# Ordering the later experts of a mixture-of-experts layer by token count on the chip, half of them with 32 places, four to a unit, their weights addressed from registers

## The chip, the cores and the metric

The kernel runs on one core of one Trainium2 chip. The metric is the device time of one execution in microseconds (us). The kernel before took 2621.86 us (median of 3 runs, 2621.36 to 2623.19).

## What is computed

A decoder layer on 512 tokens of 2048 channels in float32: two mixers, then a mixture of experts, then a gated per-layer embedding and a norm. The change is in the mixture of experts. Of the reference, what matters there:

```python
# N_GROUPS = 4, EXPERTS_PER_GROUP = 8, TOP_K = 2, D_EXPERT = 512
gi = jnp.argmax(logits_grp, axis=-1)                   # one group of 8 experts for each token
top_vals, top_idx = lax.top_k(le, TOP_K)               # two experts of that group
weights = p_sel[:, None] * jax.nn.softmax(top_vals, axis=-1)
expert_ids = gi[:, None] * EXPERTS_PER_GROUP + top_idx
# for each expert e, on the tokens xb that chose it:
hmid = jax.nn.silu(xb @ w_gate[e]) * (xb @ w_up[e])    # 2048 x 512 each
yb = hmid @ w_down[e]                                  # 512 x 2048
acc.at[idx].add(yb * wt[:, None])
```

All 32 experts' weights, 12 MiB each, are read from device memory once. With the reference's own inputs its routing gives these token counts, sorted within each group of eight: 54 49 47 45 39 38 35 31; 46 35 33 30 30 26 24 20; 52 34 33 32 32 31 28 26; 34 29 20 20 20 19 19 13.

## The kernel before, in words

The expert stage is `experts` (L1223). Every expert has 64 places for tokens (`SLOTS`); two experts form a pair, whose places fill the 128 columns of a stationary operand. For each pair there are these steps on TensorE (PE):

- `gather` (L1084) makes a one-hot matrix `G` from the tokens' ranks and multiplies the hidden state `h` by it, in a high and a low part (`ghi`, `glo`, made by ScalarE and VectorE), for two pairs (256 columns) at a time. It is a generator; one call of `next` is a **turn**, 16 matmuls of 128x256.
- `up` (L1127) multiplies the gathered tokens by `w_gate` and `w_up`, in four steps `b`, each with four weight tiles of 1 MiB. Its matmuls alternate between the two experts, 64 columns of the array each. After each `b` it calls a *window*, in which other work is put: a turn of the next gather, or a `scatter`.
- `places` (L1143) makes scale factors and the transposed one-hot matrix `GT`; `hidden` (L1163) forms the gated product; `hidden_turned` (L1171) transposes it.
- `down` (L1188) multiplies by `w_down` (8 tiles of 1 MiB), and `weighed` (L1180) splits the result in a high and a low part.
- `scatter` (L1211) adds the result back into `h`, 8 matmuls of 128x512 per step `cb`.

PE runs the program in the order written (`manual_schedule`); the other engines' order is the scheduler's. Two pairs go together: up, up, down, down. The weights come through `weight_stream` (L1029): `fill_stream` (L1064) issues each 1 MiB load on SP's queue as soon as a place is free, in the order of use. There are 16 places; four serve once, twelve (`RING` 11 and `LEFT` 1) are used again and again. `next_weights` (L1077) gives a place back when its tile is handed to PE, and the next load into it waits on SP until PE has read it. Near the end three places are kept back (`self.keep = 3`) for `project_p` (L1457), the embedding's product, whose own three inputs also lie in such places.

`count_overflow` (L1315) counts the tokens of each expert. Where one has more than its places, `overflow` (L1355) works the rest off in blocks, in a loop that sits just before the last `up` (L1267). All engines read the number of blocks (L1290) after the first two `up`. With the counts above there are none. The last pair's `down_by_columns` (L1201) alternates with `scatter` and `last_norm` (L1502); then comes `tail`.

Of the kernel before, what the change touches and what calls it, by code (L numbers as in the profile page):

```python
# [12 lines left out]
I32 = mybir.dt.int32  # L13
# [12 lines left out]
SLOTS = 64  # L26
D_POOL = 1024
# [35 lines left out]
class Layer:  # L63
# [867 lines left out]
    def router(self, pp, pm):  # L931
# [59 lines left out]
        for t in range(NT):  # L991
# [29 lines left out]
        self.aux = self.p_rt.tile([P, NT, N_EXP // 2, 3], F32, name="aux", bufs=1)  # L1021
        tt(self.aux[:, :, :, 1:3].rearrange("p t (g h) i -> p t g h i", g=4),
           og[:, :, :, None, None].to_broadcast([P, NT, 4, 4, 2]),
           wj[:, :, None, 0, :].rearrange("p t o (h i) -> p t o h i", i=2).to_broadcast([P, NT, 4, 4, 2]), op=OP.mult)
        nc.vector.tensor_copy(self.aux[:, :, :, 0], bc(rstd[:, :, None], N_EXP // 2))
        self.Mb = Mb


    def weight_stream(self):  # L1029

        a = self.a
        wp = a["w_ple_proj"][0].rearrange("(k p) (h c) -> h p k c", p=P, h=2)
        for p in range(0, N_EXP, 4):
            for q in (p, p + 2):
                for b in range(4):
                    for w in (a["w_gate"][0], a["w_up"][0]):
                        for i in range(2):
                            yield "w", w[q + i, b * T:(b + 1) * T, :].rearrange("(p j) c -> p j c", j=4), (4, T)  # L1040
                if q == N_EXP - 6:
                    yield "p", a["p"][0, 0].rearrange("(t p) c -> p t c", p=P), (NT, 256)
                    yield "p", wp[0], (2, 1024)
                if q == N_EXP - 4:
                    yield "p", wp[1], (2, 1024)
            for q in (p, p + 2):
                for k in range(4):
                    for i in range(2):
                        if q < N_EXP - 2:
                            yield "w", a["w_down"][0, q + i, k * P:(k + 1) * P, :], (D,)  # L1050
                        else:
                            yield "w", a["w_down"][0, q + i, :, k * T:(k + 1) * T].rearrange("(k p) c -> p k c", p=P), (4, T)
# [31 lines left out]
    def gather(self, pp, n):  # L1084


        nc, half = self.nc, n % 2
        home = self.p_late if half else pp
        G = home.tile([P, NT, 4, SLOTS], F32R, name=f"G{half}", bufs=1)
        m = NT if n else 1  # L1090
        for t in range(0, NT, m):
            nc.vector.tensor_tensor(G[:, t:t + m], self.slot[:, None, None, :].to_broadcast([P, m, 4, SLOTS]),  # L1092
                                    self.rank[:, t:t + m, 4 * n:4 * n + 4, None].to_broadcast([P, m, 4, SLOTS]),
                                    op=OP.is_equal)
        xe = []
        Gf = G.rearrange("p t e s -> p t (e s)")
# [8 lines left out]
        def turns():  # L1105
            ready = [parts(0), parts(1)]
            for k0 in range(0, KD, 2):
                ps = self.bank("dl")
                for i in range(2):
                    hi, lo = ready.pop(0)  # L1110
                    p = ps[:, 256 * i:256 * i + 256]
                    for t in range(NT):
                        nc.tensor.matmul(p, hi[:, t, :], Gf[:, t, :], start=t == 0, stop=False)  # L1113
                        nc.tensor.matmul(p, lo[:, t, :], Gf[:, t, :], start=False, stop=t == NT - 1)  # L1114
                if k0 + 2 < KD:
                    ready = [parts(k0 + 2), parts(k0 + 3)]
                x2 = home.tile([P, 2, 256], F32, name=f"xe{half}", bufs=KD // 2)
                for i in range(2):
                    k = k0 + i
                    nc.scalar.activation(x2[:, i, :], ps[:, 256 * i:256 * i + 256], AF.Copy,  # L1120
                                         scale=self.g_moe4[:, k // 4, k % 4:k % 4 + 1])
                    xe.append(x2[:, i, :])
                yield

        return G, xe, turns()

    def up(self, q, xe, window):  # L1127

        nc = self.nc
        c0 = (q % 2) * P  # L1130
        out = [self.bank("mm") for _ in range(2)]
        for b in range(4):
            for ps in out:
                ws = [self.next_weights() for i in range(2)]
                for j in range(4):
                    k = 4 * b + j
                    for i in range(2):
# [5 lines left out]
    def places(self, q, G):  # L1143

        nc, pp = self.nc, self.p_late
        c0 = (q % 2) * P
        Gf = G.rearrange("p t e s -> p t (e s)").bitcast(F32)
        pt = self.bank("dl")
        pa = self.bank("dl")
        for t in range(NT):  # L1150
            nc.tensor.matmul(pa[:, 0:3], Gf[:, t, c0:c0 + P], self.aux[:, t, q, :], start=t == 0, stop=t == NT - 1)
        for t in range(NT):
            nc.tensor.transpose(pt[:, t * P:(t + 1) * P], Gf[:, t, c0:c0 + P], self.ident)
        sc = pp.tile([P, 4], F32, name="sc", bufs=2)
        nc.vector.tensor_scalar(sc[:, 0:1], pa[:, 0:1], 0.5, None, op0=OP.mult)
        nc.vector.tensor_tensor(sc[:, 1:2], sc[:, 0:1], pa[:, 0:1], op=OP.mult)
        nc.vector.tensor_copy(sc[0:64, 2:3], pa[0:64, 1:2])
        nc.vector.tensor_copy(sc[64:128, 2:3], pa[64:128, 2:3])
        GT = pp.tile([P, T], F32R, name="GT", bufs=2)
# [28 lines left out]
    def down(self, hT, sc, window):  # L1188

        nc = self.nc  # L1190
        out = [self.bank("mm") for _ in range(4)]
        for k in range(4):
            window(k)
            ws = [self.next_weights() for i in range(2)]
            for cb in range(4):
                for i in range(2):
                    nc.tensor.matmul(out[cb][64 * i:64 * i + 64, :], hT[:, k, 64 * i:64 * i + 64],  # L1197
                                     ws[i][:, cb * T:(cb + 1) * T], start=k == 0, stop=k == 3)
        return [self.weighed(ps, sc) for ps in out]

    def down_by_columns(self, hT, sc, cb):  # L1201
        nc = self.nc
        ws = [self.next_weights() for i in range(2)]
        ps = self.bank("mm")
        for k in range(4):
            for i in range(2):
                nc.tensor.matmul(ps[64 * i:64 * i + 64, :], hT[:, k, 64 * i:64 * i + 64], ws[i][:, k, :],  # L1207
                                 start=k == 0, stop=k == 3)
# [14 lines left out]
    def experts(self, pp):  # L1223
        G, xe, turns = self.gather(pp, 0)
        next(turns)
        next(turns)
        left = None
        state = {}
        for n in range(N_EXP // 4):
            last = n == N_EXP // 4 - 1  # L1230
            if n == 0:
                state["turns"] = iter(())
            elif not last:
                state["next"] = self.gather(pp, n + 1)
                state["turns"] = state["next"][2]
            else:
                self.keep = 3
                state["turns"] = iter(())

            def first(b):  # L1240
                if n == 0:
                    next(turns, None)
                    next(turns, None)
                else:
                    if not last:
                        next(state["turns"], None)
                    self.scatter(b, left[0], left[1][b])
                if last:
                    if b == 0:
                        state["turns"] = self.project_p(pp)  # L1250
                    for _ in range((2, 3, 3, 4)[b]):
                        next(state["turns"])
                if b == 3:
                    state["a"] = self.places(2 * n, G)
                    if last:
                        state["b"] = self.places(2 * n + 1, G)

            out = self.up(2 * n, xe, first)
            GTa, sca = state["a"]
            hm = self.hidden(out, sca)  # L1260
            if n == 0:
                state["next"] = self.gather(pp, 1)
                state["turns"] = state["next"][2]
            if last:
                state["hTa"] = self.hidden_turned(hm)
# [4 lines left out]
            def second(b):  # L1270
                if b == 0 and not last:
                    state["hTa"] = self.hidden_turned(hm)
                if not last:
                    next(state["turns"], None)
                if n == 0:
                    next(state["turns"], None)
                if last:
                    for _ in range(3 if b else 1):
                        next(state["turns"], None)
                if b == 3 and not last:  # L1280
# [426 lines left out]
```

## Time and profile before

| what | value |
|---|---|
| median of 3 runs | 2621.86 us |
| the profiled execution's own time | 2616.97 us |
| its span, first to last instruction | 2614.9 us |
| PE busy | 2511.0 us (96%), 12358 matmul records |
| VectorE (DVE) busy, ScalarE (ACT) busy | 1148.9 us (44%), 776.7 us (30%) |
| expert stage, first `up` to last `down_by_columns` | 1361.3 to 2408 us of the span |
| read from device memory | 545.01 MB, mean 211 GB/s over the span |

Busy shares are means over the whole span, in which stages with different limits follow one another, and a busy PE is not PE at its peak, since the ends of pipelined matmuls are modelled. The expert stage is therefore read from windows, from the order of matmuls in time and from what the DMA queue waits for.

### The profile page before, as it was taken

Reading aid. Unit: us, or ns where it says so; the run is one execution under the profiler, and the core shown is the slowest. Engines: PE = TensorE matmul, PEld = TensorE weight load, DVE = VectorE, ACT = ScalarE, POOL = GpSimd, SP = SyncE. Lnnn points to the kernel's source line nnn. Section 1 sums busy time; section 2 is a strip of 40 time slices with the busy share of each in tenths; the row PEclk is TensorE's granted clock in tenths of the full one; section 3 lists DMA queues with packets and bytes.
Section 4 is the critical chain, followed back from the end, with each engine's and each line's share of the span. In section 5 each row is a group of like instructions: output and inputs, shape, how many; then the busy total and the mean of one; then the engine's idle time right before and its main releaser. Section 6 shows DMA issues by size and latency. Waiting matters only on the chain. (4 is left out here: it accounts for less than half of the span.)

```text
span 2614.9 us, 30940 instructions
## 1 busy us (share of the span) xinstructions
PE 2511.0 (96%) x12358; PEld 1720.5 (66%) x12358; DVE 1148.9 (44%) x2042; ACT 776.7 (30%) x1308; POOL 83.8 (3%) x92
## 2 busy tenths in 40 slices
PE   7999999999999999999989899999999999989998
PEld 6788888887888888877754444444444444444788
DVE  6475766765222233345453343333334333315435
ACT  4233242424222222234434222223222222113323
POOL 1001110100000000000000000000000000000001
PEclk9999999999999999999989999999999999999999
DMA  5222223234333333373237799999999999977222
GB/s 153 81 79 73 79 58 94 68 97 125 97 97 97 97 97 97 97 292 126 81 138 283 324 378 416 379 422 374 422 377 421 384 421 376 401 307 278 97 97 97
DMA packets 197975, 554.16 MB, mean 212 GB/s; under 512 B 30378, under 2 KB 127043, under 8 KB 148035
## 3 DMA queue, kind: packets, MB, share of 16 engines
q1 hardware_dynamic: 194610, 543.61, 55.4%
q10 hardware_dynamic: 2640, 4.33, 0.5%
q0 software_dynamic: 576, 4.19, 0.4%
q8 instruction: 99, 1.62, 0.2%
q14 instruction: 50, 0.40, 0.0%
HBM read 545.01 MB, written 7.08 MB: 211 GB/s over the span
## 5 line engine op out<-in xcount | busy, mean ns | idle before, releaser
L1138 PE MATMUL ps_mm<-wm,xe 128*64 128x512 f32 x2048 | 454.7, 597 | 10.6 <-DMA wm<-in_w_gate_dram 5.3
L99 PE MATMUL ps_mm<-n1h,whi 128*128 128x512 f32 x1120 | 450.4, 402 | 0.9 <-ACT whi L94 0.9
L101 PE MATMUL ps_mm<-n1h,wlo 128*128 128x512 f32 x1120 | 437.3, 391 | 1.7 <-DVE wlo L95 1.6
L100 PE MATMUL ps_mm<-n1l,whi 128*128 128x512 f32 x1120 | 437.1, 390 | 0.0
L95 DVE TENSOR_TENSOR wlo<-raw,whi 128x1024 fp32r<-128x1024 f32 x206 | 254.4, 1235 | 412.5 <-ACT whi L94 401.4
L94 ACT CAST whi<-raw 128x1024 fp32r<-128x1024 f32 x206 | 216.3, 1050 | 545.1 <-PE ps_mm L100 538.9
L1138 PEld LDWEIGHTS ps_mm<-wm,xe 128*64 128x64 f32 x2048 | 141.8, 137 | 287.0 <-issue 264.1
L95 DVE TENSOR_TENSOR glo<-h,ghi 128x512 fp32r<-128x512 f32 x128 | 137.2, 1096 | 361.1 <-ACT ghi L94 352.8
L94 ACT CAST ghi<-h 128x512 fp32r<-128x512 f32 x128 | 139.6, 1134 | 425.3 <-PE ps_dl L1113 314.2
L101 PEld LDWEIGHTS ps_mm<-n1h,wlo 128*128 128x128 f32 x1120 | 210.0, 188 | 47.3 <-DVE wlo L95 2.5
L99 PEld LDWEIGHTS ps_mm<-n1h,whi 128*128 128x128 f32 x1120 | 210.8, 188 | 40.3 <-ACT whi L94 1.3
L100 PEld LDWEIGHTS ps_mm<-n1l,whi 128*128 128x128 f32 x1120 | 210.9, 188 | 38.7
L1197 PE MATMUL ps_mm<-wm,hmT 128*64 128x512 f32 x960 | 218.8, 601 | 9.0 <-DVE eidx L1353 6.9
L1221 DVE TENSOR_TENSOR h<-h,ps_dl 128x512 f32<-128x512 f32 x256 | 160.2, 682 | 98.7 <-PE ps_dl L1219 95.9
L1197 PEld LDWEIGHTS ps_mm<-wm,hmT 128*64 128x64 f32 x960 | 66.5, 137 | 135.2 <-issue 130.0
L1113 PE MATMUL ps_dl<-G,ghi 128*128 128x256 f32 x512 | 134.2, 298 | 1.9 <-DVE G L1092 0.9
L1114 PE MATMUL ps_dl<-G,glo 128*128 128x256 f32 x512 | 128.5, 288 | 5.2 <-DVE glo L95 5.2
L1113 PEld LDWEIGHTS ps_dl<-G,ghi 128*128 128x128 f32 x512 | 99.2, 194 | 42.4 <-issue 38.9
L1218 PE MATMUL ps_dl<-yhi,GT 128*128 128x512 f32 x256 | 107.8, 421 | 14.0 <-ACT xe L1120 14.0
L1114 PEld LDWEIGHTS ps_dl<-G,glo 128*128 128x128 f32 x512 | 99.2, 194 | 7.1 <-DVE glo L95 6.9
L101 PE MATMUL ps_mm<-whi,ml 128*128 128x512 f32 x256 | 100.0, 391 | 2.1 <-DVE ml L95 2.1
L1219 PE MATMUL ps_dl<-ylo,GT 128*128 128x512 f32 x256 | 100.7, 393 | 0.0
(402 smaller groups left out, 3262.4 us busy)
## 6 DMA issues: line engine op xcount, KB each, us to landing
wm<-in_w_gate_dram SPq DMA_DIRECT2D x128, 1024.0 KB, 8.7
wm<-in_w_up_dram SPq DMA_DIRECT2D x128, 1024.0 KB, 10.2
wm<-in_w_down_dram SPq DMA_DIRECT2D x128, 1024.0 KB, 9.5
raw<-in_w_in_dram SPq DMA_DIRECT2D x144, 512.0 KB, 3.7
raw<-in_w_out_dram SPq DMA_DIRECT2D x32, 512.0 KB, 3.7
wm<-in_w_ple_gate_dram SPq DMA_DIRECT2D x16, 1024.0 KB, 5.0
raw<-in_w_up_dn_dram SPq DMA_DIRECT2D x16, 512.0 KB, 3.5
raw<-in_w_up_pool_dram SPq DMA_DIRECT2D x16, 512.0 KB, 3.6
```

The costliest lines, as they stand in the source:

```text
L94: i = self.nc.scalar.copy(hi, src)
L95: return i, self.nc.vector.tensor_tensor(lo, src, hi.bitcast(F32), op=OP.subtract)
L99: mm(ps, whi, xhi, start=start, stop=False)
L100: mm(ps, whi, xlo, start=False, stop=False)
L101: mm(ps, wlo, xhi, start=False, stop=stop)
L1113: nc.tensor.matmul(p, hi[:, t, :], Gf[:, t, :], start=t == 0, stop=False)
L1114: nc.tensor.matmul(p, lo[:, t, :], Gf[:, t, :], start=False, stop=t == NT - 1)
L1138: nc.tensor.matmul(ps[64 * i:64 * i + 64, :], xe[k][:, c0 + 64 * i:c0 + 64 * i + 64], ws[i][:, j, :], start=k == 0, stop=k == KD - 1)
L1197: nc.tensor.matmul(out[cb][64 * i:64 * i + 64, :], hT[:, k, 64 * i:64 * i + 64], ws[i][:, cb * T:(cb + 1) * T], start=k == 0, stop=k == 3)
L1218: nc.tensor.matmul(pc, GT[:, s], yh, start=True, stop=False)
L1219: nc.tensor.matmul(pc, GT[:, s], yl, start=False, stop=True)
L1221: nc.vector.tensor_tensor(d, d, pc, op=OP.add)
```

## The change

Experts 0 to 7 stay as they were. The experts 8 to 31 are sorted within their group by token count on the chip (`order_experts`, in place of `count_overflow`); `rank` and `aux` are permuted alike. The four with most tokens keep 64 places and form two pairs; the other four get 32 places each and form one unit of four. So there are 13 units (10 pairs and 3 of four) where there were 16 pairs. The weights of a sorted expert are addressed by a register that SP loads from `order`. Gathers are remade: two of 256 columns for units 0 to 3, one of 256 for units 4 and 5 and one of 128 for unit 6, then two of 384 for units 7 to 9 and 10 to 12. The order becomes up 0, up 1, down 0, up 2, down 1, and so on to up 12, down 11, down 12; a table (`plan`) says in which window a turn runs. Blocks beyond an expert's places are counted against its own 64 or 32. The overflow loop now sits between up 12 and down 11.

```diff
+LIGHT = 32
+FIRST = 8
+    def units(self):
+        u = [(0, 1), (2, 3), (4, 5), (6, 7)]
+        for g in range(FIRST, N_EXP, 8):
+            u += [(g, g + 1), (g + 2, g + 3), (g + 4, g + 5, g + 6, g + 7)]
+        return u
+    def expert(self, s):
+        if s < FIRST:
+            return slice(s, s + 1)
+        if s not in self.chosen:
+            e = self.nc.values_load(self.order[0:1, s:s + 1], engines=[mybir.EngineType.SP],
+                                    min_val=FIRST, max_val=N_EXP - 1)
+            self.chosen[s] = bass.ds(e, 1)
+        return self.chosen[s]
...
+        def ups(u):
+            for b in range(4):
+                for w in ("w_gate", "w_up"):
+                    for s in u:
+                        yield "w", rows(w, s, slice(b * T, (b + 1) * T)).rearrange("(p j) c -> p j c", j=4), (4, T)
...
-    def up(self, q, xe, window):
+    def up(self, u, xe, c0, window):
-        nc = self.nc
-        c0 = (q % 2) * P
+        nc, w = self.nc, P // len(u)
...
-                ws = [self.next_weights() for i in range(2)]
+                ws = [self.next_weights() for _ in u]
                 for j in range(4):
                     k = 4 * b + j
-                    for i in range(2):
-                        nc.tensor.matmul(ps[64 * i:64 * i + 64, :], xe[k][:, c0 + 64 * i:c0 + 64 * i + 64],
+                    for i in range(len(u)):
+                        nc.tensor.matmul(ps[w * i:w * i + w, :], xe[k][:, c0 + w * i:c0 + w * i + w],
                                          ws[i][:, j, :], start=k == 0, stop=k == KD - 1)
-            window(b)
+                window(b, h)
...
+        put(g0, *[("half", 0, b) for b in range(3)], *ups(0, range(3)))
+        put(start_2(), *ups(1), *downs(0))
+        put(start_pairs(4), *downs(1, (1, 2, 3)), *ups(3), *downs(2, (0,)))
+        put(start_light(6), *downs(2, (1, 2, 3)), *ups(4), *downs(3, (0,)))
+        for u in (7, 10):
+            put(start_all(u), *downs(u - 3, (3,)), *ups(u - 1), *downs(u - 2, (0, 1, 2)))
...
+            out = self.up(units[u], *xe[u], in_up)
+            hm[u] = self.hidden(out, at[u][1])
+            if u == 0:
+                self.order_experts(pp)
+            if u == 1:
+                self.n_blocks = self.nc.values_load(self.n_over[0:1, 0:1], min_val=0, max_val=N_EXP)
...
+            if u:
+                y[u - 1] = self.down(units[u - 1], hT[u - 1], at[u - 1][1], in_down)
...
+        def put(x):
+            tt(tmp, sel, x[:, :, None, :].to_broadcast(sh), op=OP.mult)
+            red(x, tmp, axis=AX.X, op=OP.add)
...
+        put(eights(cn))
+        put(eights(self.eidx))
+        self.order = rt.tile([P, N_EXP], I32, name="order", bufs=1)
+        nc.vector.tensor_copy(self.order, self.eidx)
+        for t in range(NT):
+            put(eights(self.rank[:, t, :]))
+            put(self.aux[:, t, 1:4, 1:9])
```

How the instructions move, at three places. **VectorE, after the first `up`.** `th` is the gated product, `sc` the scale factors, `G` the one-hot matrix, `glo` the low part for a gather, `key`, `tmp`, `pos` and `sel` the sort's tiles. Before:

```order
L1092 TENSOR_TENSOR G_10760<-slot,rank 128x1024
L1155 TENSOR_SCALAR sc<-ps_dl 128x1
L1156 TENSOR_TENSOR sc<-sc,ps_dl 128x1
L1157 COPY sc<-ps_dl 64x1
L1158 COPY sc<-ps_dl 64x1
L1167 SCALAR_TENSOR_TENSOR th_10756<-th_10756,ps_mm 128x512
L1168 SCALAR_TENSOR_TENSOR th_10756<-th_10756,sc,ps_mm 128x512
L95 TENSOR_TENSOR glo<-h,ghi 128x512 x14
```

Now:

```order
L1422 COPY cn<-ps_mm 128x32
L1217 SCALAR_TENSOR_TENSOR th_10773<-th_10773,sc,ps_mm 128x512
L1430 SCALAR_TENSOR_TENSOR key<-cn,prio 128x24
L1124 TENSOR_TENSOR G<-slot,rank 128x4x256
L1434 TENSOR_TENSOR tmp_10791<-key 128x192
L1436 TENSOR_REDUCE pos<-tmp_10791 128x24
L1438 TENSOR_TENSOR sel<-pos,eidx 128x192
L1442 TENSOR_TENSOR tmp_10791<-sel,cn 128x192
L1443 TENSOR_REDUCE cn<-tmp_10791 128x24
L1442 TENSOR_TENSOR tmp_10791<-sel,eidx 128x192
```

The first `glo` of the second gather stood right behind the gated product; now most of the sort and the whole count stand between, 21 instructions on 192 elements a partition and 25 smaller ones.

**SP, at the count of blocks.** Before:

```order
L1073 DMA wm<-in_w_down_dram 128x2048 x12
L1290 TENSOR_LOAD n_over
L1291 COMPARE_AND_BRANCH
L1344 DMA h_dram<-h 128x2048 x4
L1291 UNCONDITIONAL_BRANCH x2
L1290 ISA x2
L1073 DMA wm<-in_w_down_dram 128x2048 x4
```

Now:

```order
L1105 DMA wm<-in_w_down_dram 128x2048 x8
L1105 DMA wm<-in_w_gate_dram 128x2048 x2
L1105 DMA wm<-in_w_up_dram 128x2048 x2
L1376 TENSOR_LOAD n_over
L1377 COMPARE_AND_BRANCH
L1479 DMA h_dram<-h 128x2048 x4
L1377 UNCONDITIONAL_BRANCH x2
L1376 ISA x2
L1044 TENSOR_LOAD order
L1044 ISA x2
```

The last two rows come 14 times in a row there, ahead of the 45th weight load; the other ten register loads stand later, each ahead of its expert's first load. Every load of a sorted expert's tile has one further instruction of SP ahead of it.

**PE, a step of `up`.** Before, a pair's step with a turn of a gather behind it:

```order
L1138 MATMUL ps_mm<-wm,xe_11434 64x512 x4
L1138 MATMUL ps_mm<-wm,xe_11502 64x512 x4
L1138 MATMUL ps_mm<-wm,xe_11434 64x512 x4
L1138 MATMUL ps_mm<-wm,xe_11502 64x512 x4
L1113 MATMUL ps_dl<-G_12115,ghi 128x256
L1114 MATMUL ps_dl<-G_12115,glo 128x256
```

Now, the first step of unit 6 behind the end of down 4:

```order
L1160 MATMUL ps_dl<-G,glo 128x384
L1247 MATMUL ps_mm<-wm,hmT 64x512 x8
L1187 MATMUL ps_mm<-wm,xe_12017 32x512 x32
L1159 MATMUL ps_dl<-G,ghi 128x384
L1160 MATMUL ps_dl<-G,glo 128x384
```

A step of four experts has 32 matmuls of 32x512 where a pair's has 16 of 64x512, over twice the weights. In all, `up` and `down` go from 1536 matmuls to 960 of 64 columns and 576 of 32; gathers from 1024 matmuls to 768; scatters from 512 to 416.

## Rows read from the trace of the kernel before

**Rows 1.** The page's 40 equal slices: DMA's busy tenths and what it moved.

```profile
DMA  5222223234333333373237799999999999977222
GB/s 153 81 79 73 79 58 94 68 97 125 97 97 97 97 97 97 97 292 126 81 138 283 324 378 416 379 422 374 422 377 421 384 421 376 401 307 278 97 97 97
```

**Rows 2.** Windows: span, busy by engine (records), then clock, DMA share, GB/s.

```profile
1490.00:1500.00 10.00, 10.00 (x44) 4.13 (x44) 3.79 (x7) 0.00 (x0) 0.00 (x0) 1.00 1.01 421
2000.00:2100.00 100.00, 95.89 (x494) 45.60 (x496) 37.77 (x55) 28.78 (x41) 0.00 (x0) 1.00 0.97 397
```

**Rows 3.** Waits of SP's queue, 1480 to 2260 us: us in total, times, longest.

```profile
SPq L1073 <- PE ps_mm L1138: 424.6, 96, 9.5
SPq L1073 <- PE ps_mm L1197: 221.4, 53, 6.7
```

**Rows 4.** Timeline of PE (start us, us, work): steps of down and up.

```profile
1495.74 3.65 PE L1197 MATMUL ps_mm<-wm,hmT 128*64 128x512 f32 x16
...
1501.38 3.65 PE L1197 MATMUL ps_mm<-wm,hmT 128*64 128x512 f32 x16
1505.03 7.09 PE L1138 MATMUL ps_mm<-wm,xe 128*64 128x512 f32 x32
1516.78 7.09 PE L1138 MATMUL ps_mm<-wm,xe 128*64 128x512 f32 x32
...
1552.69 1.05 PE L1151 MATMUL ps_dl<-aux,G 128*128 128x3 f32 x8 [0.42 <-DVE h L1221]
...
1554.16 7.09 PE L1138 MATMUL ps_mm<-wm,xe 128*64 128x512 f32 x32
...
1563.68 7.09 PE L1138 MATMUL ps_mm<-wm,xe 128*64 128x512 f32 x32
1572.81 7.09 PE L1138 MATMUL ps_mm<-wm,xe 128*64 128x512 f32 x32
```

**Rows 5.** The same timeline, where the first up begins.

```profile
1361.29 7.09 PE L1138 MATMUL ps_mm<-wm,xe 128*64 128x512 f32 x32
```

**Rows 6.** The same timeline, inside a turn of a gather.

```profile
1512.50 0.28 PE L1114 MATMUL ps_dl<-G,glo 128*128 128x256 f32 x1
1512.62 0.28 PE L1113 MATMUL ps_dl<-G,ghi 128*128 128x256 f32 x1
```

**Rows 7.** Timeline of DVE and PE at the count of blocks.

```profile
1460.49 0.19 DVE L1325 COPY cn<-ps_mm 128x32 f32<-128x32 f32 x1
...
1465.16 0.18 DVE L1353 CAST eidx<-ei 128x32 f32<-128x32 int32 x1
...
1466.05 8.84 PE L1197 MATMUL ps_mm<-wm,hmT 128*64 128x512 f32 x32 [6.89 <-DVE eidx L1353]
```

**Rows 8.** DVE by line and shape in the router, 1340 to 1362 us: busy, mean ns.

```profile
L976 DVE TENSOR_TENSOR le<-lg,ge 128x128 f32<-128x128 f32 x1 | 0.3, 284 | 0.0
```

**Rows 9.** PE's wait for the weighed output when an up follows a down.

```profile
PEld ps_mm L1138 <- DVE ylo L1185: 10.5, 6, 1.9
```

**Rows 10.** SP by line, ns min/median/max: a register load, what follows it, a weight load.

```profile
L1290 SPq TENSOR_LOAD <-n_over x1: 480/480/480, 1465.2 to 1465.2; - x1
L1290 SPq FUSED_REGOPS  x1: 191/191/191, 1466.2 to 1466.2; - x1
...
L1073 SPq DMA_DIRECT2D wm<-in_w_down_dram x128: 327/378/3400, 1423.9 to 2378.3; - x128
```

**Rows 11.** Timeline of PE at the end of the stage, and the page's span.

```profile
2295.64 6.18 PE L1138 MATMUL ps_mm<-wm,xe 128*64 128x512 f32 x28
...
2320.09 4.19 PE L1138 MATMUL ps_mm<-wm,xe 128*64 128x512 f32 x12 [5.32 <-DMA wm<-in_w_gate_dram]
...
2371.57 7.09 PE L1197 MATMUL ps_mm<-wm,hmT 128*64 128x512 f32 x32
...
span 2614.9 us, 30940 instructions
```

**Rows 12.** DMA issues of the page: count, KB each, median us to landing.

```profile
raw<-in_w_in_dram SPq DMA_DIRECT2D x144, 512.0 KB, 3.7
```

More of the change, by code (lines that the diff above doesn't have):

```diff
@@ L1223, in experts @@
     def experts(self, pp):
[L1224 to L1236, printed above, removed]
-                self.keep = 3
[L1238 to L1265, printed above, removed]
@@ new lines, in experts, with gathered, spots @@
+        units = self.units()
+        last = len(units) - 1
+        xe, G = {}, {}
+        def gathered(us, G_, c0, homes):
+            parts, turns = self.gather(pp, G_, c0, homes)
+            us = iter(us)
+            for p, (_, w) in zip(parts, homes):
+                for c in range(0, w, P):
+                    xe[next(us)] = (p, c)
+            return turns
+        def spots(us, first=False):
+            widths = [(P // len(units[us[0]]), 4)]
+            if len(us) == 3:
+                widths.append((LIGHT, 4))
+            G_ = self.spots(pp, units[us[0]][0], widths, first)
+            for i, u in enumerate(us):
+                G[u] = (G_, i * P)
+            return G_
@@ new lines, in experts, with in_up @@
+        hm = {}
+        for u in range(len(units)):
+            def in_up(b, h):
+                if h == 0:
+                    turn("half", u, b)
+                    return
+                if u == 1 and b == 0:
+                    turned(0)
+                turn("up", u, b)
+                if u >= 2:
+                    self.scatter(b, at[u - 2][0], y[u - 2][b])
+                if u == last:
+                    for _ in range(3):
+                        next(rest)
+                if b == 3 and u not in at:
+                    place(u)
+                    if u in (0, 2):
+                        place(u + 1)
+            if u == last:
+                rest = self.project_p(pp)
+            if u == last - 1:
+                self.keep = 3
+            out = self.up(units[u], *xe[u], in_up)
[4 more added lines that the diff above has]
+                self.n_blocks = self.nc.values_load(self.n_over[0:1, 0:1], min_val=0, max_val=N_EXP)
+                with self.tc.If(self.n_blocks > 0):
+                    self.save_h()
+            if u == last:
+                turned(u)
@@ L1268, in experts @@
                     self.overflow(pp)
[L1270 to L1280, printed above, removed]
-                    state["b"] = self.places(2 * n + 1, G)
@@ L1298, in experts, with in_down @@
-            ya = self.down(state["hTa"], sca, third)
-            if not last:
-                yb = self.down(state["hTb"], scb, lambda k: self.scatter(k, GTa, ya[k]))
-                left = GTb, yb
-                G, xe, _ = state["next"]
+            def in_down(k):
+                if k == 2 and u < last:
+                    turned(u)
+                turn("down", u - 1, k)
+                if k == 1 and u < last and len(units[u + 1]) == 4:
+                    place(u + 1)
+                if u == last:
+                    for _ in range(3):
+                        next(rest, None)
@@ L1325, in count_overflow @@
[L1325 to L1327 removed]
+        tt(cn, cn, self.own, op=OP.subtract)
+        ts(nb, cn, 0.0, None, op0=OP.is_gt)
+        for m in range(1, T // SLOTS):
             stt(nb, cn, float(m * SLOTS), nb, op0=OP.is_gt, op1=OP.add)
```

271 lines of the change are left out of this document (164 added, 107 removed).

## The prediction

> **What bounds the kernel now.** I read the page's slices first [rows 1]: from the 22nd slice DMA is over 90% busy through the expert stage and moves 374 to 422 GB/s in turns. Windows say what that alternation is [rows 2]: where the queue is never empty it moves 421 GB/s at share 1.01, over 100 us 397 at 0.97, with PE busy 96%. So one 1 MiB tile (1.0486 MB), a chunk from here on, costs at best 1.0486/0.421 = 2.49 us, and in the middle of the stage 2.64. What holds the rest back is in SP's waits [rows 3]: of 780 us SP waits 646 for PE to have read a tile, so the places are always full and PE sets the pace. PE's steps tell why [rows 4]. A pair's `up` step of four chunks lasts 7.0 us (7.09 with the last matmul's tail); with a turn behind it 1572.81 - 1563.68 = 9.13, so a turn is 2.1; two chunks of `down` with a scatter last 1501.38 - 1495.74 = 5.6, so a scatter is 5.6 - 3.5 = 2.1; an `up` step with both 1516.78 - 1505.03 = 11.75. `places` is 1554.16 - 1552.69 = 1.5, the turned product some 0.4. Two pairs cost 48 chunks: DMA's 119.5 us against PE's 47 (up with both) + 36.5 (up with turns) + 3 + 28 + 8.4 (two downs, a scatter) + 0.8 = 124. The stage is therefore bound by PE by a few per cent, and weight traffic is close beneath. That is the key: PE can lose as much work as it likes, the stage cannot go below 2.49 us a chunk.
>
> **The change, part by part.** I lay the new program along the trace's own time. The stage begins at 1361.3 [rows 5], with 16 chunks loaded.
>
> Units 0 to 5 are still pairs. Up 0: 4 x 7.0, six turns, two `places`: 28 + 12.6 + 3 = 43.6, until 1404.9. Then the sort. Before, the count alone kept DVE from 1460.5 to 1465.2 and PE idle 6.9 us; after that PE's first 32 matmuls took 8.84 instead of 7.09, 1.8 more [rows 7]. Now 46 instructions stand ahead of the second gather's `glo`: 21 on 192 elements, at least the 0.28 us of 128 elements [rows 8] and, in proportion, at most 0.43, and 25 at 0.16 (4.7 us for 29): 10 to 13 us, and 3 us for G and the gated product. Up 1's first step covers 7.4 of it, so PE waits 6 to 9; the cover can also be better, since the first parts run meanwhile: bounds 0 and 15, I take 9, plus 1.8. Up 1: 28 + 0.4 + 8.4 + 10.8 = 47.6, until 1452.5; the read of the block count some 1; down 0: 14 + 0.4 + 8.4 = 22.8, until 1476.3 with 40 chunks used. Before, that point was 1482.4, so the sort is paid by what the count no longer costs.
>
> SP's 14 register loads there cost 0.48 + 0.19 us each [rows 10] and a little between: 10 to 12 us without a new load. The twelve chunks ahead hold over 20 us of PE's work, and PE is the slower here, so I cost this at nothing; without that cover it would be 10. Later, a further 0.19 us for each load makes 0.38 + 0.19 = 0.57 of SP's time a chunk, far under 2.49.
>
> Until unit 6 every `up` follows a `down`. An `up` needs two banks that `weighed` still reads: 10.5/6 = 1.75 us each [rows 9]; a `down` behind an `up` I give 0.5. Then: up 2: 28 + 8.4 + 3 + 1.75 = 41.2; down 1: 14.4 + 6.3 = 20.7; up 3: 47 + 1.75 = 48.8; down 2: 14.4 + 8.4 = 22.8; up 4: 47 + 1.5 + 1.75 = 50.3; down 3: 16.5; four half microseconds 2. A turn of 128 columns I price like one of 256, since matmuls follow each other at 0.12 us there [rows 6] and each still loads 128 columns of weights. Sum 202.3, until 1678.6 with 112 chunks used. That is 2.81 us a chunk, slower than now, because units 4 to 6 gather in two passes. The twelve places are then full, two in flight: 122 landed.
>
> From here DMA sets the pace. Three units (pair, pair, four) are 96 chunks, 239 us of DMA. PE needs 28 + 28 + 31 for up, 14 + 14 + 15.5 for down, 25 for three scatters, eight turns of 384 columns at 16 x 0.175 = 2.8 (between 0.12 a matmul and a scatter's 2.1/8 = 0.26), 22, and 10 for the rest: some 188. The four's step of four chunks I take at 3.9 us, which is 32 pairs of load and matmul at the 0.12 us of a turn [rows 6]; the ends are 3.5 (four experts in the time of two, per matmul half the price) and 7.0 (only two at once). PE's waits of up to 6 us between a four's steps bring the slow clock with them, 1.8 us at each restart as above [rows 7]; with twelve places it hides under the loads. Up 12's last chunk is the 363rd: 241 x 2.49 = 600, so 2278.7.
>
> **The end.** In up 12 only six or seven places turn over (three kept or taken for `project_p`, its inputs in two or three). PE frees four at a time while three are under way: I add 4 us (0 to 31, the upper end if each of the eight steps had 3.9 us with no load under way). The last step: 3.9, until 2286.6. Before, PE needed from the end of up 14's matmuls (2301.8) to 2320.1 for window, count of places and loop [rows 11]; now there are two `places` and one product less, 18.3 - 3.0 - 1.4 = 14. From 2320.1 to the end of that pair's `down`, 2378.7, it was 58.6, of which the `up` 28 that no longer lies behind the loop: 30.6. From there to the end of the span 2614.9 - 2378.7 = 236.2, which stays: seven of the 24 chunks left are under way at the loop, the rest lands in some 50 us while PE has as much to do. 2286.6 + 14 + 30.6 + 236.2 = 2567.4.
>
> **Sum.** The span falls by 47.5 us. Against the profiled execution's own 2616.97 that is 2569.5; the median of the runs lies 4.9 above that execution, so I forecast **2574 us**. Without the sort's wait (11), the four's places (4) and the bank waits (9) it would be 2550.
>
> A rule of the skill speaks against any gain at all. Rows 2 show 421 GB/s into one core. The Trainium skill (DMA: Bandwidth & Descriptors, Specifications) gives a limit of about 358 GB/s for one core's share of device memory. (The skill's HBM Reference adds that a core alone measures about 425.) By the limit a chunk would cost 2.93 us, the 241 chunks 106 us more, and the kernel would end at 2680, slower than before; the trace disagrees, since it holds 421 where the queue is full.
>
> **The rivals.**
> 1. *Fours run two at a time.* For it: the trace has only two experts side by side. Against it: those two do overlap fully, 32 matmuls of 0.59 us in 7.09 us [rows 4]. Units 6 and 9 still hide it (56 + 8 + 11 = 75 of 80 us); in unit 12 a step then takes 7.0 + 4.5 to refill, or 7.0 + 6.3 with a window's work, 12.4 instead of 10.2 on average, 18 us, and four steps of `down_by_columns` 3.1 more each: 2574 + 31 = 2605. The Trainium skill (TensorE: Matmul & The Clock Gate, Part 3) reports 3.07 times for four tiles, which would make the step 4.6 us and the sum some 4 us more; no run so far shows it.
> 2. *DMA does not hold 421.* If 397 over 100 us [rows 2] is DMA's own pace and not PE's, a chunk costs 2.64 and 241 of them 36 more: 2610. Against it: SP's waits name PE.
> 3. *An expert of a light half gets more than 32 tokens* and the overflow loop runs. It decides at the 33rd token. Third group's fifth count is exactly 32; the others are 30 and 20. One block loads 64 tiles of 256 KB in three places; a 512 KB load takes 3.7 us to land [rows 12], so 64 x 3.7/3 = 79 at least and 237 one at a time. I take 79: 2653, slower than before.
> 4. *Loads by register are slow to issue.* If SP needs more than 2.49 us a chunk it becomes the bound; from 2.69 the gain is gone. The longest issue in the trace took 3.4 us [rows 10], which on all 241 chunks would be 2793, but the median is 0.38.
>
> **How the numbers follow.** A measurement of this kernel tells about 0.2% (5 us) from no change. The forecast gets 0.74, rival 1 0.07, rival 2 0.07; rivals 1 and 2 together, or two further waits of some 20 us, bring it back to the old time, 0.04; rival 3 gets 0.05 and rival 4 0.03. Faster: 0.74 + 0.07 + 0.07 = 0.88; same 0.04; slower 0.08. The range runs from 2550 (the sum's lower bounds) to 2612 (rivals 1 and 2 each on its own).
>
> **What would show it.** Right: from about 1680 on, windows at 415 GB/s or more without dips, until some 2280; PE idle in the fours' steps, waiting for DMA; matmul records of 32 columns, 64 of them (an `up` step's two halves) in near 8 us; one wait of PE for DVE in up 1; no row of `overflow`. Wrong: SP waiting for PE as long as before, DMA below 400 after 1700, SP's issue rows above 2 us, or fours' matmuls one or two at a time.

## The result and the profile after

The changed kernel takes 2575.77 us (median of 4 runs, 2573.61 to 2578.76) against 2621.61 for the kernel before beside it: a ratio of 0.9827, with an interval of 0.9810 to 0.9844. Forecast were 2574. The profiled execution took 2573.61, its span is 2571.8. Its slices answer to [rows 1]: from the 23rd slice on DMA is over 90% busy in twelve of thirteen (the 8 is the stretch that PE still bounds), and where it alternated between 374 and 422 GB/s it stands at 419 to 421 for eight slices.

```profile
PE   7999999999999999999989999998988898879998
DMA  5232223233333333355235999899999999988322
GB/s 156 82 81 66 80 66 89 61 102 123 91 97 98 99 98 94 95 209 217 90 123 220 396 414 356 339 420 421 421 421 420 421 419 420 404 319 294 106 91 99
```

The windows of the changed kernel, stretch by stretch (answering to [rows 2]; the last three numbers of a row are the granted clock, DMA's share and GB/s):

```profile
core 0: us, PE busy (x) PEld busy (x) DVE busy (x) ACT busy (x) POOL busy (x), PEclk, DMA share, GB/s
1480.00:1580.00 100.00, 96.20 (x492) 47.05 (x490) 44.90 (x64) 30.96 (x43) 0.00 (x0) 1.00 0.98 398
1580.00:1680.00 100.00, 97.01 (x488) 46.31 (x486) 36.51 (x49) 27.86 (x44) 0.00 (x0) 0.97 0.86 344
1680.00:1780.00 100.00, 89.61 (x476) 38.97 (x472) 30.74 (x48) 20.89 (x34) 0.00 (x0) 0.97 1.01 421
1980.00:2080.00 100.00, 86.26 (x447) 39.73 (x447) 30.23 (x38) 24.64 (x44) 0.00 (x0) 0.97 1.01 421
2180.00:2280.00 100.00, 79.28 (x388) 30.27 (x386) 19.28 (x37) 11.75 (x18) 0.00 (x0) 0.91 0.99 400
2280.00:2340.00 60.00, 50.99 (x242) 26.21 (x246) 14.30 (x20) 12.26 (x19) 0.00 (x0) 0.87 0.77 292
```

From 1680 to 2180 PE's share falls from 96 and 97 to between 86 and 91%, while DMA stays at 419 to 421 GB/s: the bound has passed from PE to DMA. In up 12 (2180 on) PE's share is 79%, the granted clock 0.91, and DMA at 400. Over 1680 to 2280 DMA moved 417 GB/s, before 397. SP's waits there (engine, line, what it waited for: us, times, longest), answering to [rows 3], say the same; before, SP waited 502 us for PE's two lines there, and for DMA not at all:

```profile
SPq L1105 <- PE ps_mm L1187: 147.8, 62, 10.0
SPq L1105 <- PE ps_mm L1247: 109.7, 35, 8.2
SPq L1105 <- DMA wm<-in_w_up_dram: 75.0, 44, 2.9
SPq L1105 <- DMA wm<-in_w_gate_dram: 70.5, 40, 2.0
SPq L1105 <- DMA wm<-in_w_down_dram: 59.1, 39, 2.0
```

PE's timeline in up 12, the last four, shows it tile by tile (start, duration, shape, count, idle before and what ended it). Two records, a tile's first matmul (`up`'s 1024 float32 matmuls left 2048 records, two each), come every 2.49 us, the pace of DMA, after 1.4 us of waiting; behind a window's other work the tiles have gathered, and 34 to 36 records follow at once. The last lines are the way through the loop to the last `down` but one:

```profile
2202.46 1.04 PE L1187 MATMUL ps_mm<-wm,xe 128*32 128x512 f32 x2 [0.34 <-DMA wm<-in_w_gate_dram]
2204.95 1.04 PE L1187 MATMUL ps_mm<-wm,xe 128*32 128x512 f32 x2 [1.45 <-DMA wm<-in_w_gate_dram]
2207.43 6.02 PE L1187 MATMUL ps_mm<-wm,xe 128*32 128x512 f32 x30 [1.44 <-DMA wm<-in_w_gate_dram]
...
2249.20 4.84 PE L1187 MATMUL ps_mm<-wm,xe 128*32 128x512 f32 x36
...
2281.16 5.76 PE L1187 MATMUL ps_mm<-wm,xe 128*32 128x512 f32 x26 [3.37 <-DMA wm<-in_w_up_dram]
...
2301.38 0.80 PE L101 MATMUL ps_dl<-pw,pT 128*128 128x512 f32 x1 [7.85 <-issue]
...
2306.45 3.65 PE L1247 MATMUL ps_mm<-wm,hmT 128*64 128x512 f32 x16
...
2326.04 3.65 PE L1247 MATMUL ps_mm<-wm,hmT 128*64 128x512 f32 x16
```

The prediction's milestones beside the trace:

| | predicted | measured |
|---|---|---|
| up 2 begins | 1476.3 | 1467.0 |
| up 5 begins | 1678.6 | 1667.5 |
| end of up 12's matmuls | 2286.6 | 2286.9 |
| PE goes on behind the loop | 2300.6 | 2301.4 |
| down 11's matmuls end | 2331.2 | 2329.7 |
| span | 2567.4 | 2571.8 |

The twelve products of `project_p` in down 11's first window come right behind the loop; down 11's own first matmul is at 2306.5.

### The profile page after: what moved, and what is told of

It is laid out like the page before. It is cut to its first block, busy times and chain, and to the rows that moved or that the text cites. A ratio compares the mean times of both kernels' runs of the same rounds, so it can differ in the third digit from the quotient of the medians.

```text
span 2571.8 us, 30607 instructions
## 1 busy us (share of the span) xinstructions
PE 2419.3 (94%) x11958; PEld 1653.6 (64%) x11958; DVE 1082.3 (42%) x1967; ACT 726.7 (28%) x1255; POOL 83.6 (3%) x92
## 5 line engine op out<-in xcount | busy, mean ns | idle before, releaser
L1187 PE MATMUL ps_mm<-wm,xe 128*64 128x512 f32 (+1 forms) x2048 | 428.6, 634 | 47.2 <-DMA wm<-in_w_up_dram 39.9
L1187 PEld LDWEIGHTS ps_mm<-wm,xe 128*64 128x64 f32 (+1 forms) x2048 | 122.3, 132 | 326.0 <-issue 226.8
L1271 DVE TENSOR_TENSOR h<-h,ps_dl 128x512 f32<-128x512 f32 x208 | 130.3, 681 | 237.7 <-PE ps_dl L1269 236.5
L1247 PE MATMUL ps_mm<-wm,hmT 128*64 128x512 f32 (+1 forms) x896 | 199.8, 639 | 23.5 <-DMA wm<-in_w_down_dram 17.9
L96 ACT CAST ghi<-h 128x512 fp32r<-128x512 f32 x96 | 109.7, 1174 | 244.4 <-PE ps_dl L1159 233.9
L1247 PEld LDWEIGHTS ps_mm<-wm,hmT 128*64 128x64 f32 (+1 forms) x896 | 55.2, 135 | 141.1 <-issue 98.9
L1159 PE MATMUL ps_dl<-G,ghi 128*128 128x256 f32 (+2 forms) x384 | 112.7, 318 | 2.5 <-DVE h L1271 1.5
L1160 PE MATMUL ps_dl<-G,glo 128*128 128x256 f32 (+2 forms) x384 | 108.5, 307 | 0.9 <-DVE glo L97 0.9
L102 PE MATMUL ps_mm<-wlo,mh 128*128 128x512 f32 x256 | 100.2, 391 | 0.0
L101 PE MATMUL ps_mm<-whi,mh 128*128 128x512 f32 x256 | 100.1, 391 | 0.0
## 6 DMA issues: line engine op xcount, KB each, us to landing
wm<-in_w_up_dram SPq DMA_DIRECT2D x128, 1024.0 KB, 14.6
```

What stands on the lines that cost most here:

```text
L96: i = self.nc.scalar.copy(hi, src)
L101: mm(ps, whi, xhi, start=start, stop=False)
L102: mm(ps, whi, xlo, start=False, stop=False)
L1159: nc.tensor.matmul(p, hi[:, t, :], G[:, t, c0:c0 + n], start=t == 0, stop=False)
L1160: nc.tensor.matmul(p, lo[:, t, :], G[:, t, c0:c0 + n], start=False, stop=t == NT - 1)
L1187: nc.tensor.matmul(ps[w * i:w * i + w, :], xe[k][:, c0 + w * i:c0 + w * i + w], ws[i][:, j, :], start=k == 0, stop=k == KD - 1)
```

## The experiments

Ratios are to the kernel before, timed beside each kernel; 0.001 is 2.6 us, an interval about 0.0017 to either side. The changed kernel has 0.9827. Of each edit the lines that matter are shown; `...` stands for the rest.

**A four's matmuls two at a time.** In `up`, and alike in `down` and `down_by_columns`:

```
-  nc.tensor.matmul(ps[w * i:w * i + w, :], xe[k][:, c0 + w * i:c0 + w * i + w],
...
+  r = 64 * (i * w // 64)
+  nc.tensor.matmul(ps[r:r + 64, :], xe[k][:, c0 + r:c0 + r + 64],
...
```

> Every matmul of a four takes the 64 columns of two experts, so that only two run at once; the products of the two add up in the same 64 places (the result of the fours is left out by that). DMA, order, gathers and everything else stay. Theory (DMA sets the pace from 1660 to 2280, PE has some 50 us of slack in each three units): units 6 and 9 hide it, only the last four and its four steps by columns show it, by the sum of rival 1 in the prediction 31 us: 2595 to 2612. Rival: PE sets the pace in the middle too: each four costs 28 us more in up and 14 in down, three of them 126 us: 2690 to 2702, with DMA under 400 GB/s from 1700 on.

Measured: 0.9897 (0.9881 to 0.9914), 2591.0 us, some 18 us over the changed kernel by the ratios and just under the range expected. DMA kept 417 to 421 from 1680 to 2180, so units 6 and 9 did hide the work added to them, as the theory says, and the rival with 126 us falls. What showed was half of the 31: up 12's matmuls ended at 2293.4 instead of 2286.9 (6.5), and from down 11's start to the last column block's matmuls it took 66.9 instead of 58.9 (8.0).

**Less work for PE, fewer bytes for DMA.** The pair that names the bound: half the products of the scatters in up 7 to up 11 are left out, or 16 loads.

```
-  nc.tensor.matmul(pc, GT[:, s], yl, start=False, stop=True)
+  if not half:
+      nc.tensor.matmul(pc, GT[:, s], yl, start=False, stop=True)
...
```

> In up 7 to up 11 a scatter leaves out the product with the low part (the output of units 5 to 9 is a little less exact): 80 matmuls of 512 columns and their loads, some 1 us a scatter, 20 us of PE's work in the middle. Theory: DMA sets the pace there and PE only waits longer: 0 to 3 us, ratio 0.9815 to 0.9835. Rival: PE sets the pace: 20 us, ratio 0.975.

```
-  for w in ("w_gate", "w_up"):
+  for w in ("w_gate",) if u[0] in (16, 24) else ("w_gate", "w_up"):
...
```

> Units 7 and 10 (pairs of the middle) don't load their w_up: the second half step takes the tiles of w_gate again, PE does all its matmuls, and 16 tiles of 1 MiB fewer are read (the result of these four experts is left out). Theory: DMA sets the pace from 1657 on, so 16 x 2.49 = 40 us go, less what PE's own work then holds back, 28 to 40 us under the changed kernel: ratio to the kernel before 0.967 to 0.972 (the changed kernel's is 0.983). Rival: PE sets the pace there, or SP's issuing: then nothing goes, 0.981 to 0.984.

Measured: 0.9840 (0.9821 to 0.9858) without the products, nothing gained, PE only idler (84.80 us busy in 1980:2080 instead of 86.26):

```profile
1980.00:2080.00 100.00, 84.80 (x430) 36.32 (x422) 27.26 (x35) 23.02 (x40) 0.00 (x0) 0.95 1.01 421
```

Without the loads 0.9743 (0.9726 to 0.9760), 22 us less: bytes shorten the time and PE's work doesn't. The 22 fall short of the 28 to 40: up 7 and up 10 keep PE for some 36 us (28 and four scatters), which lay under the 40 of sixteen tiles and stands out over the 20 of eight. So PE bounds there, and the queue shows it: these three windows lack some 20 us of transfers at 421 GB/s (an estimate from their rates), about what is missing.

```profile
1780.00:1880.00 100.00, 91.73 (x491) 40.22 (x487) 27.50 (x41) 18.56 (x32) 0.00 (x0) 0.98 0.94 386
1980.00:2080.00 100.00, 89.63 (x444) 42.41 (x437) 28.17 (x37) 22.45 (x40) 0.00 (x0) 0.97 0.97 399
2080.00:2180.00 100.00, 91.46 (x441) 34.76 (x440) 23.82 (x49) 8.92 (x14) 0.00 (x0) 0.98 0.95 392
```

**Unit 6's gather later, or together with that of 4 and 5.** Two ways to relieve PE before the stream takes over. The first:

```
-  put(start_light(6), *downs(2, (1, 2, 3)), *ups(4), *downs(3, (0,)))
+  put(start_light(6), *ups(5), *downs(4))
```

> Unit 6's gather is made in up 5 and down 4 instead of down 2, up 4 and down 3: eight turns, some 14 to 17 us of PE's work, move past 1651, where the queue stood empty for some 7 us because all twelve places were full. Theory: up to there PE sets the pace, from there DMA. The tiles in the places cover the moved turns, so the stream runs ahead by at most what the twelve places allow: when up 6 began, some eight of the twelve were full, so at most four tiles, 10 us, are to be had: 4 to 10 us less than the changed kernel, 2566 to 2572. Rival 1: PE sets the pace through up 6 all the same and the turns cost there what they cost before: within 3 us, 2573 to 2579. Rival 2: DMA sets the pace from early on, PE's order is of no account: likewise within 3 us; then the queue in the window 1580 to 1680 moves 421 GB/s or stays at 344 as it was, which tells the two apart.

The second, with `home == "ring"` for a place of the weights:

```
-  yield from gathered([u, u + 1], spots([u, u + 1, u + 2]), 0, [("xe0", 256)])
+  yield from gathered([u, u + 1, u + 2], spots([u, u + 1, u + 2]), 0, [("xe0", 256), ("ring", P)])
...
-  put(start_light(6), *downs(2, (1, 2, 3)), *ups(4), *downs(3, (0,)))
...
```

> Units 4, 5 and 6 are gathered in one pass of 384 columns instead of two of 256 and 128; unit 6's part lies in one of the twelve places of the weight ring until up 6 is done, nothing is left out. Theory: PE sets the pace until up 6 starts at 1728; there eight turns of 128 columns (1.5 to 2 us each) go and eight turns grow by some 0.6: 7 to 11 us less work of PE ahead of the stretch that DMA bounds, and so 6 to 11 us under the changed kernel, ratio 0.9785 to 0.9805. Rival: DMA already sets the pace there, or the ring of eleven costs what is saved: 0.982 to 0.984.

Measured: 0.9819 (0.9802 to 0.9835) for the move, not told apart from the changed kernel; 0.9801 (0.9784 to 0.9817), some 7 us less with an interval that still overlaps the changed kernel's, for one pass. The windows of the moved gather show the first rival, PE pacing up 6 all the same: 419 GB/s where there were 344, and then 360 where there were 421, so over 300 us (1480 to 1780) 383 + 419 + 360 against 398 + 344 + 421, the same bytes, and up 6 began at 1727.1 instead of 1728.0.

```profile
1580.00:1680.00 100.00, 96.63 (x462) 40.74 (x460) 32.02 (x48) 17.86 (x26) 0.00 (x0) 1.00 1.01 419
1680.00:1780.00 100.00, 88.78 (x506) 44.99 (x506) 36.80 (x54) 31.74 (x52) 0.00 (x0) 0.91 0.89 360
```

In the single pass up 6 began at 1714.2 instead of 1728.0, but up 12's matmuls ended only 7.2 us sooner. The bytes of the whole early stretch fit that; of the changed kernel, the single pass and the run with more sorting below:

```profile
1361.00:1780.00 419.00, 400.97 (x2093) 191.03 (x2092) 163.22 (x257) 128.09 (x187) 0.00 (x0) 0.98 0.92 373
```

```profile
1361.00:1780.00 419.00, 398.53 (x2000) 186.17 (x1999) 148.04 (x246) 110.34 (x172) 0.00 (x0) 0.99 0.93 378
```

```profile
1361.00:1780.00 419.00, 397.48 (x2067) 188.46 (x2070) 181.89 (x316) 125.15 (x181) 0.00 (x0) 0.98 0.91 367
```

378 - 373 = 5 GB/s over 419 us are 2.1 MB, at 421 GB/s 5 us: the span fell by 5.4. (Kernels that leave this stretch alone have 372 to 375, so 3 us of it are chance; the moved gather has 377.) By these rows what counts of an early gain is the tiles that landed by it, and twelve places bound how far they run ahead.

**More sorting.** Three idle copies of each step of the sort:

```
+  for _ in range(3):
+      tt(tmp, sel, x[:, :, None, :].to_broadcast(sh), op=OP.mult)
+      red(pos, tmp, axis=AX.X, op=OP.add)
```

> Each of the ten pairs of product and sum that put counts, numbers, ranks and weights in their new order is made four times (three into a tile that nobody reads): 60 more instructions of 192 elements on DVE, some 22 us, in unit 1. Theory: the sort is off the path, because only the two first parts of the second gather are needed before it and the later parts stand between its instructions in DVE's order: PE waits at most 3 us and the ratio stays at 0.9815 to 0.9845. Rival, the prediction's own step: the sort stands ahead of the parts that PE needs; its end at 1417 moves to 1439, PE needs the next part at 1422.5, so PE stops for some 17 us in a stretch that PE bounds, of which at least half reaches the end: ratio 0.986 to 0.990.

Measured: 0.9836 (0.9819 to 0.9853), not told apart from the changed kernel, and the rival's 0.986 lies outside. For 18.7 us more work on DVE (181.89 against 163.22 in the rows above) PE waited once for a part of the gather, 4.0 us, a little over the 3 that the theory allowed (the changed kernel, 0.7, second):

```profile
PE ps_dl L1160 <- DVE glo L97: 4.0, 1, 4.0
```

```profile
PE ps_dl L1160 <- DVE glo L97: 0.7, 1, 0.7
```

The profiled span is 6.1 us longer, as its early bytes above say (367 against 373 GB/s); the timed runs don't resolve that.

**Fixed addresses.** `expert` returns its slice for every unit:

```
-  if s < FIRST:
+  if s < N_EXP:
       return slice(s, s + 1)
```

> The order found on the chip still sets places and weights of the tokens, but every weight tile is read at a fixed address (expert s at place s), so SP has no register loads and no address arithmetic; the experts after the eighth get the weights of others of their group, so their result is left out. Theory: SP issues far faster than 2.49 us a tile, the price of the registers is 0: ratio 0.9815 to 0.9845, as the changed kernel. Rival: the 14 loads in unit 1 (10 us) or the slower issues cost time: 5 us or more under it, ratio 0.981 or less.

Measured: 0.9801 (0.9786 to 0.9816), below the theory's range and within the rival's, with intervals that overlap the changed kernel's. The traces don't bear the rival's mechanism out: 372 GB/s over 1361 to 1780 against 373, 421 in the middle as before. They differ behind 2180: 409 GB/s against 400 in 2180:2280, where the runs that keep up 12 as it is scatter from 393 to 406, and, more clearly, at the overflow loop. There SP stood 4.3 us in the loop's own line and PE 5.45; the changed kernel and the six runs of this section that keep the loop as it is have 11.3 to 13.8 and 7.8 to 9.8. (First line: fixed addresses; second: the changed kernel.)

```profile
SPq L1382 <- SPq L1382: 4.3, 2, 2.5
```

```profile
SPq L1382 <- SPq L1382: 11.3, 2, 7.6
```

So register addresses cost 0 to 7 us, and by this one trace what they cost shows at the loop, not in issuing; why the loop holds SP longer with them is open.

**The loop over overflow blocks.** It makes no turn with these inputs. First without it, then, with the `places` of the units behind it read sooner, behind up 11 and behind up 10:

```
   if u == last:
       turned(u)
+  if u == last - 1:
+      turned(u)
       self.overflow_setup(pp)
       with self.tc.For_i(0, self.n_blocks, 1):
...
```

> The loop over overflow blocks is left out, with its setup; no block of a crowded expert is computed (with these inputs there is none, so the loop makes no turn). Theory: the last part, from up 12's last step to the last column block, is a chain of PE with weights enough under way, so what the loop holds up falls out: in the changed kernel's trace PE stands still from 2293.5 to 2301.4, about 8 us, and takes 1.7 us more for the twelve matmuls behind it: 8 to 14 us less than the changed kernel, 2562 to 2568. Rival: the stream of weights sets the end too (24 tiles after the 363rd are 60 us); then PE only waits longer for w_down and the time stays within 3 us, 2573 to 2579.

> The loop over overflow blocks stands behind up 11 instead of up 12, nothing is left out. Theory: there DMA sets the pace and some nine tiles (22 us) are under way, so PE's stop of 8 to 10 us uses slack that PE has anyway, and the whole of the loop's price at the end goes: the same as with no loop, 2562 to 2568, within 3 us of that run. Rival: three places are kept free there, the loop stops SP from issuing, the queue runs empty and the stop is only moved: 2573 to 2579.

> The overflow loop stands behind up 10, before any place is kept free; places of units 11 and 12 are read one unit sooner, nothing is left out. Behind up 11 the loop held SP for 17.7 us with about six tiles under way, so that the queue stood empty for some 9 us. Theory: with twelve under way (30 us) the queue outlasts the stop, PE has slack there, and the loop's price at the end is saved as in the run without it: 5 to 10 us under the changed kernel, ratio 0.979 to 0.981. Rival: PE or SP loses at any place what it loses at the end: 0.982 to 0.984, with a gap in the queue near 2080.

Measured: 0.9801 (0.9785 to 0.9818), some 7 us less without it, just under the 8 to 14 expected (12 in the profiled spans; the intervals overlap); 0.9828 and 0.9842 for the two other places, nothing won: my theory of a place with slack fell twice. The trace of the last of them says why. PE stood 12.28 us, SP in the loop's own line 19.3 us, and DMA ran dry before either went on (second block: the rate in 40 slices of 2100 to 2122):

```profile
2106.26 1.09 PE L1225 MATMUL ps_dl<-ident,th 128*128 128x128 f32 x4 [1.93 <-DVEq L1388]
2119.63 5.93 PE L1248 MATMUL ps_mm<-wm,hmT 128*32 128x512 f32 x32 [12.28 <-SPq L1388]
```

```profile
GB/s 432 402 462 417 402 417 432 462 387 417 417 462 372 447 402 447 417 417 402 402 447 358 417 417 387 253 268 253 283 253 104 60 30 0 0 0 15 0 0 0
```

The changed kernel shows it at its place, 2284 to 2304, the queue at nothing from 2298 on, SP in the loop's line for the 11.3 us shown above and PE idle until 2301.4:

```profile
GB/s 360 442 475 279 180 49 164 229 377 410 410 410 459 377 442 459 410 426 377 442 475 377 442 475 393 426 393 131 0 16 0 0 0 33 16 0 0 0 16 0
```

```profile
PE ps_dl L101 <- issue: 7.8, 1, 7.8
```

So the price is not a stop that finds cover somewhere: wherever the loop stood, the queue ran empty about when the program went on. That SP waits there for its loads to land fits the rows; it was not taken apart further. Hence the last question, a branch around it:

```
-  with self.tc.For_i(0, self.n_blocks, 1):
-      self.overflow(pp)
+  with self.tc.If(self.n_blocks > 0):
+      with self.tc.For_i(0, self.n_blocks, 1):
+          self.overflow(pp)
```

> The overflow loop stands where it stood, inside a branch that is taken only if there is a block; nothing is left out. The runs with the loop moved showed what it costs: engines leave it only after SP has seen all loads land (behind up 10 PE stood 12.3 us and the queue ran empty wherever the loop was put). Theory: it is the loop that drains the queue, and the branch of unit 1, beside which PE showed no wait and the queue only a dip of 2 us, does not: so a branch not taken costs near nothing and the time is that of the kernel with no loop, ratio 0.979 to 0.981. Rival: any control flow that waits for all engines drains the queue: ratio 0.982 to 0.985.

> Units 4 to 6 gathered in one pass, as in the run that tried it alone (some 8 us under the changed kernel), and the overflow loop inside the branch; nothing is left out. Theory: the first shortens the part that PE bounds, the second the end, and DMA holds its pace between them, so the two add up: 14 to 18 us under the changed kernel, ratio 0.976 to 0.978. Rival: the branch saves nothing: ratio 0.980; or what is won ahead is lost to the ring in the last four: 0.979 to 0.980.

Measured: 0.9785 (0.9770 to 0.9800) with the branch, as without the loop or a little better; 0.9779 (0.9765 to 0.9792) with the single pass as well, 2563.99 us, the fastest kernel that leaves nothing out. Both intervals lie wholly under that of the changed kernel, by some 11 and 13 us at the middle, so the branch's gain is shown; the two can't be told from each other, so the sum of both is not. The theory holds in half: at the branch PE waited 3.76 us instead of 7.8, but SP still stood 11.9 us in its line, and the queue still fell to nothing, for 2 us.

```profile
2294.49 0.77 PE L101 MATMUL ps_dl<-pw,pT 128*128 128x512 f32 x1 [3.76 <-PEq L1382]
```

## Why the prediction was right, and where not

- **What bounds it.** DMA from 1657 on: shown for the middle by the pair of runs with less work and fewer bytes. PE until then: by the queue that stood empty for it (below) and PE's 96 and 97%. 421 GB/s (419 in the last window) held from 1680 to 2180; the sign of 415 or more until 2280 failed behind that, with 400. The limit of about 358 GB/s that the Trainium skill gives (DMA: Bandwidth & Descriptors, Specifications) is exceeded in this trace; the time by it, 2680, was 104 us off.
- **The sort** is the term that failed: taken at 9 us of waiting and 1.8 of ramp, it cost PE nothing: PE's one wait for DVE in unit 1, 0.7 us, comes at 1444, long after. The step set all of its 46 instructions ahead of the second gather's parts. But the first two parts were made before it, PE had two steps and a turn to do, and needed the next part only at 1422.5, while DVE made its `glo` from 1417.0 to 1418.1. With the block count's 1 us, which wasn't there either, 11.8 us were priced that did not come; up 2 began 9.3 early and up 5 11.1. On DVE and PE, in order of time:

```profile
1415.30 7.09 PE L1187 MATMUL ps_mm<-wm,xe 128*64 128x512 f32 x32
...
1416.95 0.14 DVE L1475 CAST n_over<-cum 128x1 int32<-128x1 f32 x1
1417.02 1.09 DVE L97 TENSOR_TENSOR glo<-h,ghi 128x512 fp32r<-128x512 f32 x1
...
1422.32 0.39 PE L1159 MATMUL ps_dl<-G,ghi 128*128 128x256 f32 x1
```

- **The stream.** DMA's rate in 40 slices of 1640 to 1700 shows where it takes over: the queue stood empty from 1650 to 1657, with 104 tiles used and twelve in their places, 116 landed.

```profile
GB/s 426 426 431 426 437 437 98 0 0 0 0 55 306 426 437 437 426 431 415 421 415 421 415 426 415 421 410 421 431 415 415 426 415 431 421 426 415 426 410 437
```

  From 1657 on 247 more at 2.49 make 2272 for the 363rd, against 2278.7 predicted; the last step began at 2281.2. So the stream was 7 us ahead of the forecast. Where the sum had 4 us for the squeeze of the ring, 9 were lost, some 5 of them in 2180:2280 (400 GB/s instead of 421). The last step took 5.8 instead of 3.9: its granted clock read 0.63 (2281 to 2287) after a wait of 3.4 us, and in the run without the loop the same 26 records took 3.6 at 1.00. That up 12 ended 0.3 us from the forecast is these errors meeting.
- **The four's step**, taken at 3.9, is 3.5: two of them, 64 records, in 7.07 us, where 32 of a pair took 7.09 [rows 4]. The 3.07 times of the Trainium skill (TensorE: Matmul & The Clock Gate, Part 3) are its figure for four row tiles, while a four lies in column tiles; it would make the step 4.6 by the estimate of the prediction, and the row is below that.

```profile
1728.04 7.07 PE L1187 MATMUL ps_mm<-wm,xe 128*32 128x512 f32 x64 [0.82 <-DVE ylo L1234]
```

- **The loop** was taken at 14 us, 18.3 less two `places` and a product; to the same point, PE's first matmul behind the loop, it is 14.5 (2286.9 to 2301.4). That is luck in part: PE stood 7.85 us there where it had stood 5.3 before [rows 11], and the work beside it was shorter than the sum had it. The step priced PE's work; what the runs show at this place is a queue run dry.
- **The end.** From there to the end of down 11 it took 28.3 us instead of 30.6. From that to the span's end 242.1 instead of 236.2 [rows 11]: the third column block waited 2.19 us for its weights, and its other 26 records then took 5.32 us instead of 3.62, with a granted clock of 0.72 in 2349 to 2355. The step had let the rest of the weights land while PE was busy. The loop is not the whole of it, since without it the same block waited 1.66 us.

```profile
2345.36 1.66 PE L1258 MATMUL ps_mm<-wm,hmT 128*32 128x512 f32 x6
2349.20 5.32 PE L1258 MATMUL ps_mm<-wm,hmT 128*32 128x512 f32 x26 [2.19 <-DMA wm<-in_w_down_dram]
```

- **The rivals.** No row of an overflow block appears (rival 3), SP's issues are not the bound (rival 4: their median is 0.33 us; the register addresses, put at nothing, may cost the 0 to 7 us found at the loop), and DMA's own pace is 421 and not 397 (rival 2). Rival 1 was priced too high: 18 us where the prediction had 31.
- **Slips in its readings.** DMA is over 90% busy from the 24th slice on [rows 1], not from the 22nd. The 4.7 us of [rows 7] were 24 instructions and not 29, so 25 cost some 5 us and not 4. The bank waits in the sum are 7.3 us (three of 1.75 and 2), not the 9 that the range's lower end takes off. None of them moves the forecast by more than 2 us.

In sum: 49.0 us less at the end of that last `down` (2378.7 to 2329.7), 5.9 given back after it, 43.1 in the span. The mechanism, a bound that passes from PE to DMA at 2.49 us a tile, was right. That the median came within 2 us was luck: terms missed by up to 12 us either way and cancelled, and the span's 4.4 us over the forecast were partly offset because the profiled run lay 2.2 us under the median and not 4.9.

## What to carry to other kernels

Before pricing what an engine saves, work out what the next bound allows: a tile costs 2.49 us however little PE does, so of the PE work taken out of the middle only the few per cent down to that floor were to be had. In such a stretch count bytes landed by a given time, not when a unit starts; moving work within it won nothing here that can be told from chance. And a loop over a count read on the chip cost time here even with no turn, wherever it stood: price the stop of the load queue with it, and try a branch around it, which won some 11 us.

## What had not been expected

- The loop empties the load queue wherever it stands: the queue fell to nothing in all three places tried, and PE stood 7.8 us at the end, 7.7 behind up 11 and 12.3 behind up 10, where the most loads were under way.
- With the queue never empty a load takes longer from issue to landing, a median of 14.6 us for `w_up` where it was 10.2 before, at a higher rate: here the landing time was no sign of a slower DMA.
- Four matmuls of 32 columns share PE as fully as two of 64: 64 records of a four took 7.07 us, 32 of a pair 7.09.
